# The last norm's reciprocal root: from GpSimd's power to a ScalarE root and a Newton step, with the last token tile multiplied in two column halves

## The chip, the cores and the metric

The kernel runs on one core of a Trainium2 chip. The metric is device microseconds (us) of one execution of the whole program; before the change the median of three runs is 1013.2 us. The engines are PE (TensorE: matmuls, with PEld for its weight loads), DVE (VectorE), ACT (ScalarE), POOL (GpSimd) and SP (SyncE, which here only issues transfers). Each works through its own queue in order, and waits in that queue on semaphores that other engines or transfers raise.

## The reference

One layer of a latent backbone: a short gated convolution, then a SwiGLU feed-forward, each behind an RMS norm that is modulated by a conditioning vector, each added to the residual, and a last RMS norm. 1024 tokens, model dimension 1024, hidden dimension 2816, all float32.

```python
def rmsnorm(x, g):
    return x * lax.rsqrt(jnp.mean(x * x, axis=-1, keepdims=True) + EPS) * g

sh1, sc1, g1, sh2, sc2, g2 = jnp.split(silu(c) @ ada_w + ada_b, 6, axis=-1)
x = x + g1 * short_conv_mixer(modulate(rmsnorm(x, norm1_g), sh1, sc1), ...)
gate, up = jnp.split(modulate(rmsnorm(x, norm2_g), sh2, sc2) @ ffn_w_in, 2, axis=-1)
x = x + g2 * ((silu(gate) * up) @ ffn_w_out)
return rmsnorm(x, final_g)
```

The change touches only the last two lines: the end of the feed-forward's output product, the residual and the last norm.

## The kernel before

**Products.** Each float32 operand is split in a high and a low half (`hi` by a cast on ACT, `lo` by a subtraction on DVE, L74), and a product takes three matmuls (`TERMS`: high by high, high by low, low by high). The large products are made in Winograd's form of Strassen's scheme: seven products of quarter matrices in place of eight.

**The output product** (matmuls on L999, sums `zP`) is the last 209 us of the program. Its seven products run in the order P1, P5, P6, P2, P7, P3, P4 (the table `PRODUCTS`). Each goes over 11 tiles `k` of half the hidden dimension, for four tiles of 128 tokens; each token tile has one PSUM bank of 128x512. The operands `a3h`, `a3l` (tokens) and `w3h`, `w3l` (weights) of two `k` at a time are loaded by SP, cast on ACT and completed on DVE, some steps ahead of PE. A product's `epilogue` for a token tile is issued while the next product's matmuls run: it works the sums into `top[t]` (tokens of the upper half) and `bot[t]` (lower half). P3's epilogue finishes the four `top` tiles during P4, P4's finishes the four `bot` tiles.

**The end.** P4 (`final`) takes the token tiles 0 to 2 as a group over all `k`, then the last tile (`t == TH - 1`) alone: 33 matmuls of 128x512 into the fourth bank, so that the epilogues of the first three tiles run beside it. Then that tile's own epilogue runs with nothing beside it: DVE multiplies by `g2` and adds the residual (`residual_part`: `mul`, `add`), ACT squares and sums (`AF.Square` with `accum_out`, L920), DVE multiplies the tile by the norm's gain `fg` into `zf` meanwhile, `rstd_sum` adds the sums of the left and the right half (`z_ss`), and `rstd_of` takes the mean and its power -0.5 in two instructions on GpSimd (`z_ms` L193, `z_r` L195). With `z_r`, DVE scales the left half (L974), ACT the right half (L977), and SP (L978) and ACT (L979) issue the two transfers to `out_dram`. The other seven tiles use `rstd_of` too. The `top` tiles' transfers are issued by GpSimd (L965).

**What sets the order.** A scheduler orders each engine's queue from the order of the program text and its own costs; `tc.issue_after(mm)` pins a piece of work behind a matmul. Waits between engines are set for a whole tile: a writer of a bank waits for the readers of that bank. At the end of the program (L1060) each engine has a DRAIN, and then all meet at a barrier, which GpSimd's queue gathers.

Of the kernel before, what the change touches and what calls it, by code (L numbers as in the profile page):

```python
# [16 lines left out]
H = 512          # tokens of a half, and the most columns of one product  # L17
GRID_W = 64
EPS = 1e-6
# (stationary, moving) halves of a float32 product: all but low * low  # L20
# [4 lines left out]
def trunk_kernel(ctx: ExitStack, tc: tile.TileContext, x, c, ada_w, ada_b, norm1_g, norm2_g,  # L25
# [4 lines left out]
    KD = D // P              # tiles of the model dimension  # L30
    KH = KD // 2
    NT = T // P              # tiles of tokens
    TH = H // P              # of them in a half
# [61 lines left out]
    def rows_of(name, vectors):  # L95
        """Vectors of 128, a row each; of each (first row, queue, source) a run of them."""
        rows = t2(name)[:, :P]
        nc.vector.memset(rows, 0.0)
        for r, queue, v in vectors:
            v = v.rearrange("o (k p) -> (o k) p", p=P)  # L100
            queue.dma_start(rows[r:r + v.shape[0], :], v)
        return rows
# [22 lines left out]
    aw = ada_w.rearrange("(k p) (j d) -> p k j d", p=P, j=6)  # L125

    class Ada:
        """Columns d0..d0+w of nj of the six vectors from j0: first each partition's own rows of
        ada_w, then their sum over the partitions."""
# [35 lines left out]
        def columns(self, i, g, scale, shift):  # L165
            """g * (1 + scale) and shift of its i-th tile of the model dimension, as columns."""
            ps, k, j0 = self.ps[i], self.d0 // P + i, self.j0
            nc.vector.tensor_scalar(scale[:, k:k + 1], ps[:, 1:2], ab1[:, (j0 + 1) * KD + k:(j0 + 1) * KD + k + 1],
                                    g[:, k:k + 1], op0=ALU.add, op1=ALU.mult)
            nc.vector.tensor_scalar(shift[:, k:k + 1], ps[:, 0:1], ab[:, j0 * KD + k:j0 * KD + k + 1], None, op0=ALU.add)  # L170

        def row(self, to, bias=False):
            """The sums, to their rows in DRAM; of one vector with its bias."""
# [36 lines left out]
    xT = [[t_s(f"xT{h}_{kp}", [P, 2, H]) for kp in range(KH)] for h in range(2)]  # L210

    class Tokens:
# [5 lines left out]
        def squares(self):  # L218
            # the squares themselves go where the other half's tokens come later
            self.ss = tiny(f"x{self.t}_ss")  # L220
            nc.scalar.activation(xT[1][self.i].rearrange("p k t -> p (k t)"), self.x, AF.Square, accum_out=self.ss)
# [38 lines left out]
    # ---- the convolution's input product, channels in partitions; its first channel tiles take the  # L260
    # first half of the tokens as the columns of scale and shift arrive ----
    C0 = 2
    JS = (2, 1, 0)          # hv, gate_c, gate_b
# [27 lines left out]
    def convolve(ct, u, cv):  # L291
        """Rows of the grid in u; taps of channel tile ct."""
# [9 lines left out]
    def gated0(ct, h):  # L302
        """gate_c * hv of a first channel tile and a half of the tokens."""
        u = first[ct, h] = t2(f"u{ct}_{h}")
        nc.scalar.copy(u, ps0[ct, 2, h])
        mul(u, ps0[ct, 1, h], u)
# [8 lines left out]
    # A: tokens by dimension, B: its dimension by two tiles of columns; 1 and 2 are halves.  # L315
    class Pair:
        """The products of two tiles of columns."""
# [16 lines left out]
        def weights(self, tile=t_wop):  # L334
            (b11, b21), (b12, b22) = [(raw[:, :KH, :], raw[:, KH:, :]) for raw in self.raw]
            sub(b11, b12, b11)                      # T1
            self.weight("P5", b11, tile)
            self.weight("P3", b22)
            sub(b12, b22, b12)                      # T3
            sub(b22, b22, b11)                      # T2  # L340
            self.weight("P6", b22, tile)
            self.weight("P7", b12, tile)
            sub(b21, b21, b22)                      # -T4
# [20 lines left out]
        def after(self, name, ps):  # L364
# [4 lines left out]
            elif name == "P6":  # L369
                nc.scalar.copy(self.u2, ps)                     # P1 + P6  # L370
            elif name == "P7":
                self.u3 = t2(f"u3_{self.name}")
                nc.scalar.copy(self.u3, ps)                     # P1 + P6 + P7
# [15 lines left out]
    def in_turn(pairs, count, between=None):  # L389
        """Pairs one after the other, but a product of the next one in between where one of a pair  # L390
        waits for its bank's sum to be read; the last one has its own products there."""
# [20 lines left out]
    class Mix(Pair):  # L412
        """Channel tiles ct and ct + 1 of hv (2), gate_c (1) or gate_b (0)."""
# [49 lines left out]
    def operands(raw):  # L463
        """The sums of quarters, from raw tiles by half of the tokens; what they are needed in order."""
# [5 lines left out]
        for kp in range(2):  # L470
            sub(s1[kp], s1[kp], raw[0][kp])                             # S2
            operand("S2", kp, s1[kp])
        yield
        for kp in range(2):
            sub(raw[1][kp], raw[0][kp], raw[1][kp])                     # S3
            operand("S3", kp, raw[1][kp])
        yield
        for kp in range(2):
            sub(raw[0][kp + 2], raw[0][kp + 2], s1[kp])                 # S4
# [10 lines left out]
    with in_order(ENG.SP, ENG.DVE, ENG.Activation, ENG.PE):  # L490
# [41 lines left out]
        while r:  # L532
            then = piece() if spans else None
            n = KD // len(p.ks)         # rows of the next piece to each of these
# [67 lines left out]
    def finish_piece(p=None):  # L602
        """After a product of p."""
# [50 lines left out]
    def v_tile(t, parts):  # L654
        """All channels of a tile of tokens, loaded where its low half comes."""
# [111 lines left out]
    # The output product's operands: a half of the tokens by tiles of the hidden dimension.  # L767
# [17 lines left out]
    def spill_sums(i):  # L785
        a, at = acts.pop(i), acts.pop(i + FH)
        sx, sy = t_s(f"asx_{i}", [P, 2, H]), t_s(f"asy_{i}", [P, 2, H])
        add(sx[:, 0, :], a[:, 1, :], at[:, 1, :])               # S1
        sub(sx[:, 1, :], sx[:, 0, :], a[:, 0, :])               # S2
        sub(sy[:, 0, :], a[:, 0, :], a[:, 1, :])                # S3  # L790
        sub(sy[:, 1, :], at[:, 0, :], sx[:, 1, :])              # S4
# [46 lines left out]
    queued = []  # L838

    def load(o, src):  # L840
        """In this order on their queue."""
# [7 lines left out]
    def wsource(pname, k, n):  # L849
        """The raw weight quarter of a product, for tiles k..k+n of the hidden dimension; T1 is there ahead of P5."""  # L850
# [9 lines left out]
        if pname == "P2":  # L860
            o = part("21")
            sub(tchain[k], o, tchain[k])                     # -T4
# [3 lines left out]
        if pname == "P7":  # L866
            o = part("22")
            sub(o, o, part("12"))                            # T3
            return o
        if pname == "T1":  # L870
            tchain[k] = part("12", t_s)
            sub(tchain[k], tchain[k], raw11.pop(k))          # T1, for P5
        elif pname == "P6":
            sub(tchain[k], part("22"), tchain[k])            # T2
# [31 lines left out]
    # The rows of C of a tile of tokens in each half: (C11, C12) and (C21, C22), from their parts.  # L906
# [8 lines left out]
    def residual_part(t, z, to, x1, cols):  # L915
        """x1 + g2 * z and its sum of squares."""
# [5 lines left out]
    parts = cst.tile([P, 2 * NT], F32, name="parts")          # sums of squares: left, then right halves  # L922
# [6 lines left out]

    def rstd_sum(t):  # L930
        s = tiny(f"z{t}_ss")
        add(s, parts[:, 2 * t:2 * t + 1], parts[:, 2 * t + 1:2 * t + 2])
        return rstd_of(s, f"z{t}")

    def epilogue(pname, t, z):
# [6 lines left out]
        elif pname == "P6":  # L942
            nc.scalar.copy(top[t][:, R], z)                               # P1 + P6
        elif pname == "P2":
            add(top[t][:, L], z, top[t][:, L])                            # C11
            add(top[t][:, R], top[t][:, R], bot[t][:, R])                 # P1 + P6 + P5
            if t < 2:
                top_left(t)
        elif pname == "P7":
            nc.scalar.copy(bot[t][:, L], z)                               # P1 + P6 + P7  # L950
            x1 = x1b[t] = x1_part(t + TH, "x1", slice(0, D), t_s)
            zr = bot[t][:, R]
            add(zr, bot[t][:, L], zr)                                     # C22
# [4 lines left out]
        elif pname == "P3":  # L958
            zr = top[t][:, R]
            add(zr, z, zr)                                                # C12  # L960
# [4 lines left out]
            nc.gpsimd.dma_start(out[t * P:(t + 1) * P, :], top[t])  # L965
        else:                                                             # P4: z is C21
            zl, rows = bot[t][:, L], out[(t + TH) * P:(t + TH + 1) * P]
            residual_part(t + TH, z, zl, x1b[t][:, L], L)
            if t == TH - 1:
                zf = t2("zf")  # L970
                mul(zf, zl, fg[:, L])
            r = rstd_sum(t + TH)
            if t == TH - 1:
                nc.vector.tensor_scalar(zl, zf, r, None, op0=ALU.mult)  # L974
            else:
                nc.vector.scalar_tensor_tensor(zl, zl, r, fg[:, L], op0=ALU.mult, op1=ALU.mult)
            nc.scalar.mul(bot[t][:, R], bot[t][:, R], r)  # L977
            nc.sync.dma_start(rows[:, L], zl)  # L978
            nc.scalar.dma_start(rows[:, R], bot[t][:, R])  # L979
# [3 lines left out]
    for pname in PRODUCTS:  # L983
# [12 lines left out]
        def steps(t, k):  # L996
            a, w = ops[k // 2]
            for i, (ai, wi) in enumerate(TERMS):
                mm = nc.tensor.matmul(zs[t], lhsT=a[ai][:, k % 2, t * P:(t + 1) * P], rhs=w[wi][:, k % 2, :],  # L999
# [5 lines left out]
        for k, n in ksteps:  # L1005
# [13 lines left out]
            if pname == "P6" and k == 4:  # L1019
                g2, fg = t_s("g2", [P, D]), t_s("fg", [P, D])  # L1020
                load(g2, g_rows[1][0].broadcast_to([P, D]))
                load(fg, final_g.rearrange("(o d) -> o d", o=1).broadcast_to([P, D]))
        low(FH - 1)
# [4 lines left out]
        if final:  # L1028
            for t in range(group):
                epilogue(pname, t, zs[t])  # L1030
            with tc.issue_after(mm):
                for k in range(FH):
                    steps(TH - 1, k)
            epilogue(pname, TH - 1, zs[TH - 1])
# [30 lines left out]
```

## Time and profile before

| | us |
|---|---|
| runs (three) | 1011.79, 1013.2, 1013.22; median 1013.2 |
| span of the profiled execution | 1010.4 |
| PE busy in the span | 983.7 (97%) |
| DVE / ACT / POOL busy | 724.5 / 443.6 / 90.4 |
| PE on L999, share of the chain that ended last | 21% |

The profiled execution has no time of its own beside its span; the span is 2.8 us below the median of the runs. PE works nearly throughout, so most of the program's length is PE's; the last matmul begins at 996.36 us. An engine's rows give a start, a duration, the line, the operation, and the output and inputs by the program's names; "idle before <-releaser" is what its engine waited for.

### The profile page before, as it was taken

Reading aid. Unit: us, or ns where it says so; the run is one execution under the profiler, and the core shown is the slowest. Engines: PE = TensorE matmul, PEld = TensorE weight load, DVE = VectorE, ACT = ScalarE, POOL = GpSimd, SP = SyncE. Lnnn points to the kernel's source line nnn. Section 1 sums busy time; section 2 is a strip of 40 time slices with the busy share of each in tenths; the row PEclk is TensorE's granted clock in tenths of the full one; section 3 lists DMA queues with packets and bytes.
Section 4 is the critical chain, followed back from the end, with each engine's and each line's share of the span. In section 5 each row is a group of like instructions: output and inputs, shape, how many; then the busy total and the mean of one; then the engine's idle time right before and its main releaser. Section 6 shows DMA issues by size and latency. Waiting matters only on the chain.

```text
span 1010.4 us, 12038 instructions
## 1 busy us (share of the span) xinstructions
PE 983.7 (97%) x4395; PEld 812.8 (80%) x4395; DVE 724.5 (72%) x1051; ACT 443.6 (44%) x711; POOL 90.4 (9%) x172
## 2 busy tenths in 40 slices
PE   5999999999999999999999999999999999999994
PEld 5788888887888878888888888888888888888883
DVE  6879798887945799677665665665665765777973
ACT  7684333333535575243333333333333353634642
POOL 2010000000011110110110110110110100000021
PEclk8999999999999999999999999999999999999997
DMA  9921456443875232454431431431326954578432
GB/s 308 354 68 57 128 149 208 123 149 121 250 219 182 84 105 84 137 176 135 146 115 53 146 115 53 146 115 53 126 74 218 378 183 147 187 260 294 145 134 104
DMA packets 137386, 157.36 MB, mean 156 GB/s; under 512 B 6724, under 2 KB 100016, under 8 KB 137328
## 3 DMA queue, kind: packets, MB, share of 16 engines
q1 hardware_dynamic: 126944, 124.27, 39.2%
q0 software_dynamic: 9728, 31.26, 8.4%
q10 hardware_dynamic: 656, 1.08, 0.3%
q8 instruction: 34, 0.56, 0.2%
q14 instruction: 24, 0.20, 0.1%
HBM read 123.80 MB, written 32.78 MB: 155 GB/s over the span
## 4 chain that ended last, share of the span: by engine, by line
PE 90%; DVE 4%; DMA 2%; SPq 1%; issue 1%; ACT 1%; POOL 0%; POOLq 0%; ACTq 0%; DVEq 0%
PE X_f L356 23%; PE zP L999 21%; PE Z_f L356 12%; PE X_m L356 8%; PE y L670 7%; PE Y_f L356 6%; PE u L286 6%; PE Z_m L356 4%; PE Y_m L356 2%; DMA ada_w<-in_ada_w_dram 1%; DVE ada_acc L152 1%; PE x1T L643 1%; DVE BP_f L74 1%; SPq L140 1%; DMA wr_m<-in_conv_w_in_dram 1%
## 5 line engine op out<-in xcount | busy, mean ns | idle before, releaser
L74 DVE TENSOR_TENSOR BP_f<-wr_f,BP_f 128x512 fp32r<-128x512 f32 x154 | 104.8, 688 | 60.7 <-ACT BP_f L83 58.9
L83 ACT CAST BP_f<-wr_f 128x512 fp32r<-128x512 f32 x154 | 93.9, 621 | 85.2 <-PE Z_f L356 51.6
L999 PE MATMUL zP<-w3l_P,a3h_P 128*128 128x512 f32 x308 | 119.8, 389 | 0.0
L999 PE MATMUL zP<-w3h_P,a3l_P 128*128 128x512 f32 x308 | 119.8, 389 | 0.0
L999 PE MATMUL zP<-w3h_P,a3h_P 128*128 128x512 f32 x308 | 118.4, 389 | 0.0
L999 PEld LDWEIGHTS zP<-w3l_P,a3h_P 128*128 128x128 f32 x308 | 57.8, 188 | 12.1
L999 PEld LDWEIGHTS zP<-w3h_P,a3l_P 128*128 128x128 f32 x308 | 57.8, 188 | 12.0
L999 PEld LDWEIGHTS zP<-w3h_P,a3h_P 128*128 128x128 f32 x308 | 57.8, 188 | 11.9
L74 DVE TENSOR_TENSOR a3l_P<-a3l_P,a3h_P 128x1024 fp32r<-128x1024 f32 (+1 forms) x42 | 47.3, 1133 | 27.8 <-ACT a3h_P L889 27.8
L83 ACT CAST BP_m<-wr_m 128x512 fp32r<-128x512 f32 x63 | 37.7, 620 | 59.0 <-DVE wr_m L74 32.2
L152 DVE SCALAR_TENSOR_TENSOR ada_acc<-ada_w,cols,ada_acc 128x512 f32<-128x512 f32 (+1 forms) x88 | 61.7, 711 | 2.4 <-ACT ada_acc L148 0.8
L356 PE MATMUL X_f<-A11h,BP_f 128*128 128x512 f32 x176 | 57.7, 390 | 0.0
L356 PE MATMUL X_f<-AS3h,BP_f 128*128 128x512 f32 x176 | 57.7, 389 | 0.0
L356 PE MATMUL X_f<-AS2h,BP_f 128*128 128x512 f32 x176 | 57.6, 389 | 0.0
L356 PE MATMUL X_f<-A22h,BP_f 128*128 128x512 f32 x176 | 57.6, 389 | 0.0
L356 PE MATMUL Z_f<-AS4h,BP_f 128*128 128x512 f32 x176 | 57.6, 389 | 0.0
L356 PE MATMUL Y_f<-A12h,BP_f 128*128 128x512 f32 x176 | 57.5, 389 | 0.0
L356 PE MATMUL Z_f<-AS1h,BP_f 128*128 128x512 f32 x176 | 57.4, 389 | 0.0
L74 DVE TENSOR_TENSOR BP_m<-wr_m,BP_m 128x512 fp32r<-128x512 f32 x63 | 42.4, 688 | 14.5 <-ACT BP_m L83 14.1
L670 PE MATMUL y<-woh,vh_t 128*128 128x512 f32 x128 | 50.4, 394 | 0.0
L670 PE MATMUL y<-woh,vl_t 128*128 128x512 f32 x128 | 49.9, 390 | 0.0
L670 PE MATMUL y<-wol,vh_t 128*128 128x512 f32 x128 | 49.9, 390 | 0.0
(273 smaller groups left out, 2239.1 us busy)
## 6 DMA issues: line engine op xcount, KB each, us to landing
wr_f<-in_ffn_w_in_dram SPq DMA_DIRECT2D x44, 512.0 KB, 4.1
ada_w<-in_ada_w_dram SPq DMA_DIRECT2D x64, 256.0 KB, 5.9
w_P<-in_ffn_w_out_dram SPq DMA_DIRECT2D x30, 512.0 KB, 5.7
a3l_P<-ad_S SPq DMA_DIRECT2D x20, 512.0 KB, 6.5
wr_m<-in_conv_w_in_dram SPq DMA_DIRECT2D x18, 512.0 KB, 5.3
ad<-a POOLq DMA_DIRECT2D x33, 256.0 KB, 2.6
ada_w<-in_ada_w_dram SPq DMA_DIRECT2D x16, 512.0 KB, 3.9
a3l_P<-ad SPq DMA_DIRECT2D x15, 512.0 KB, 3.8
```

Source lines behind the costliest of these rows:

```text
L74: return nc.vector.tensor_tensor(o, a, b, op=ALU.subtract)
L83: nc.scalar.copy(hi, raw)
L140: self.last_load = nc.sync.dma_start(raw[:, :, j, :], aw[:, k0:k0 + kk, j0 + j, d0:d0 + w]).ins
L152: nc.vector.scalar_tensor_tensor(acc, self.rows[k], by, acc, op0=ALU.mult, op1=ALU.add)
L286: nc.tensor.matmul(ps0[ct, j, h], lhsT=w0[k][wi][:, j, ct * P:(ct + 1) * P], rhs=h_of(k, h)[hi], start=(k == 0 and i == 0), stop=(k == KD ...
L356: mm = nc.tensor.matmul(ps, lhsT=w[:, wi, 2 * kp + kk, :], rhs=A[aname, kp][hi][:, kk, :], start=(first and kp == 0 and kk == 0 and i == 0 ...
L643: nc.tensor.transpose(ps2[:, i * P:(i + 1) * P], xn[:, k * P:(k + 1) * P], ident)
L670: mm = nc.tensor.matmul(ys[t][n], lhsT=vt[t][vi][:, k, :], rhs=wo[k][wi][:, n * H:(n + 1) * H], start=(k == 0 and i == 0), stop=(k == KD - ...
L999: mm = nc.tensor.matmul(zs[t], lhsT=a[ai][:, k % 2, t * P:(t + 1) * P], rhs=w[wi][:, k % 2, :], start=(fresh and k == 0 and i == 0), stop= ...
```

## The change

- `rstd_sum` adds the two sums and `D * EPS` in one DVE instruction, and `rsqrt` makes the reciprocal root: ACT's `Sqrt` (L940), then on DVE a reciprocal, `r * r * s`, `1.5 - 0.5 *` that, and a product (one Newton step). For eight tiles that is 8 instructions of 128x1 on ACT, 40 on DVE in place of 8, and none on GpSimd in place of 16. The mean's 1/D goes into `fg`, which GpSimd multiplies once by the root of D when it is loaded.
- The `top` tiles' transfers move from GpSimd's queue to ACT's.
- The last token tile's 33 matmuls of 512 columns become 66 of 256 columns: first all `k` for the left 256 columns, then all `k` for the right, in the same bank. `LastTile.half` does the residual part of each half; `rest` does the norm.

```diff
     def rstd_sum(t):
         s = tiny(f"z{t}_ss")
-        add(s, parts[:, 2 * t:2 * t + 1], parts[:, 2 * t + 1:2 * t + 2])
-        return rstd_of(s, f"z{t}")
+        nc.vector.tensor_scalar(s, parts[:, 2 * t:2 * t + 1], parts[:, 2 * t + 1:2 * t + 2], D * EPS,
+                                op0=ALU.add, op1=ALU.add)
+        return rsqrt(s, f"z{t}")
+
+    def rsqrt(s, name):
+
+        r, e = tiny(f"{name}_r"), tiny(f"{name}_e")
+        nc.scalar.activation(r, s, AF.Sqrt)
+        nc.vector.reciprocal(r, r)
+        nc.vector.scalar_tensor_tensor(e, r, r, s, op0=ALU.mult, op1=ALU.mult)
+        nc.vector.tensor_scalar(e, e, -0.5, 1.5, op0=ALU.mult, op1=ALU.add)
+        mul(r, r, e)
+        return r
...
-            nc.gpsimd.dma_start(out[t * P:(t + 1) * P, :], top[t])
+            nc.scalar.dma_start(out[t * P:(t + 1) * P, :], top[t])
...
+    class LastTile:
+
+
+        def __init__(self, t, zs):
+            self.t, self.zs, self.zf = t, zs, t2("zf")
+            self.ss, self.sums = [tiny(f"zl_ss{i}") for i in range(2)], tiny("zl_sums")
+
+        def half(self, i):
+            c = slice(i * H // 2, (i + 1) * H // 2)
+            t, z, x1 = self.t, bot[self.t][:, c], x1b[self.t][:, c]
+            mul(z, self.zs[i][:, c], g2[:, c])
+            add(z, z, x1)
+            nc.scalar.activation(x1, z, AF.Square, accum_out=self.ss[i])
+            mul(self.zf[:, c], z, fg[:, c])
+            if i == 0:
+                right = 2 * (t + TH) + 1
+                nc.vector.tensor_scalar(self.sums, self.ss[0], parts[:, right:right + 1], D * EPS,
+                                        op0=ALU.add, op1=ALU.add)
+
+        def rest(self):
+            t, s = self.t, tiny("zl_s")
+            rows = out[(t + TH) * P:(t + TH + 1) * P]
+            add(s, self.ss[1], self.sums)
+            r = rsqrt(s, "zl")
+            nc.vector.tensor_scalar(self.zf, self.zf, r, None, op0=ALU.mult)
+            nc.scalar.mul(bot[t][:, R], bot[t][:, R], r)
+            nc.sync.dma_start(rows[:, L], self.zf)
...
+                nc.gpsimd.tensor_scalar(fg, fg, D ** 0.5, None, op0=ALU.mult)
...
         if final:
             for t in range(group):
                 epilogue(pname, t, zs[t])
-            with tc.issue_after(mm):
-                for k in range(FH):
-                    steps(TH - 1, k)
-            epilogue(pname, TH - 1, zs[TH - 1])
+            last = LastTile(TH - 1, [zs[TH - 1]] * 2)
+            for i in range(2):
+                with tc.issue_after(mm):
+                    for k in range(FH):
+                        mm = steps(TH - 1, k, cols=slice(i * H // 2, (i + 1) * H // 2))
+                last.half(i)
+            last.rest()
```

Where the instructions stand now, at three places. The first is GpSimd's queue from the last spill of the feed-forward's activations (L795) to the end of the program, as a piece of the difference (the part for the tiles z2 to z7 repeats what is shown).

```order
 L778 DMA ad_3072<-a_6234 128x512
 L795 DMA ad_S_3077<-asy_6245 128x512
-L193 TENSOR_SCALAR z_ms<-z_ss 128x1
-L195 TENSOR_TENSOR z_r<-z_ms,mhalf 128x1
-L965 DMA out_dram<-top_6492 128x1024
...
-L1060 UNCONDITIONAL_BRANCH
-L1060 ISA
+L1059 TENSOR_SCALAR fg<-fg 128x1024
+L1100 UNCONDITIONAL_BRANCH
+L1100 ISA
```

GpSimd's last work of its own is now the scaling of `fg`, which stands in the middle of the output product; the norms and the four transfers are gone from its queue. The second place is the seam between the two column halves, first on PE (`zP_3` is the last tile's bank, `_10` the last `k`, `_0` the first).

```order
L1034 MATMUL zP_3_6243<-w3h_P_10_7748,a3h_P_10_7744 128x256
L1034 MATMUL zP_3_6243<-w3l_P_10_7749,a3h_P_10_7744 128x256
L1034 MATMUL zP_3_6243<-w3h_P_10_7748,a3l_P_10_7745 128x256
L1034 MATMUL zP_3_6243<-w3h_P_0_7561,a3h_P_0_7557 128x256 [waits DVE_49]
L1034 MATMUL zP_3_6243<-w3l_P_0_7562,a3h_P_0_7557 128x256
```

PE's first matmul of the right columns now waits for DVE, for the instruction that reads the left columns out of the shared bank; before, no matmul of the last tile had such a wait. That instruction stands in DVE's queue here (fifth row below; `bot_6692` and `bot_6730` are the tiles 0 and 1, `bot_6811` the last; the `z` names are the norms' 128x1 columns).

```order
L943 TENSOR_SCALAR z_e<-z_e 128x1 [waits DVE_49]
L80 TENSOR_TENSOR z_r<-z_r,z_e 128x1 [waits DVE_49]
L982 SCALAR_TENSOR_TENSOR bot_6692<-bot_6692,z_r,fg 128x512 [waits DVE_49]
L941 RECIPROCAL z_r<-z_r 128x1 [waits Activation_49]
L80 TENSOR_TENSOR bot_6811<-zP_3_6243,g_6732 128x256 [waits PE_49]
L942 SCALAR_TENSOR_TENSOR z_e<-z_r,z_ss 128x1 [waits DVE_49]
```

It comes behind the first tile's norm and the second one's reciprocal, and ahead of the rest of the second one's. The third place is ACT's queue in the middle of P4 (`w3h_P_10` is the last weight cast that PE needs; `top_6492` is tile 0, `top_6562` tile 2).

```order
L889 CAST a3h_P_10_7744<-a3l_P_10_7745 128x512 [waits DMAHW3_49,PE_49,Activation_49]
L883 CAST w3h_P_10_7748<-w_T_12_10_6433 128x512 [waits PE_49]
L940 ACT_TABLE_LOAD
L940 ACTIVATE z_r<-z_ss 128x1 [waits DVE_49] x2
L920 ACTIVATE x1r_7682,parts<-top_6562 128x512 [waits DMAHW0_49,DVE_49]
L976 ACTIVATE top_6492<-top_6492,z_r 128x512 [waits DVE_49]
L977 DMA out_dram<-top_6492 128x1024 [waits DVE_49,Activation_49]
```

Before, the first `top` tile's scaling followed the last weight cast directly; now a load of ACT's function table and two roots stand between, and a transfer's issue behind it.

## Rows read from the trace of the kernel before

**Rows 1.** The page: the length of the profiled execution.
```profile
span 1010.4 us, 12038 instructions
```

**Rows 2.** Busy time in three stretches of the end; idle engines show 0.00.
```profile
core 0: us, PE busy (x) PEld busy (x) DVE busy (x) ACT busy (x) POOL busy (x), PEclk, DMA share, GB/s
...
1001.00:1004.00 3.00, 0.00 (x0) 0.00 (x0) 0.00 (x0) 0.00 (x0) 0.00 (x0) 0.50 0.47 175
1004.00:1008.00 4.00, 0.00 (x0) 0.00 (x0) 0.00 (x0) 0.00 (x0) 0.00 (x0) 0.50 0.00 0
1008.00:1010.40 2.40, 0.00 (x0) 0.00 (x0) 0.00 (x0) 0.00 (x0) 0.00 (x0) 0.50 0.00 0
```

**Rows 3.** The program's last line, L1060: ns min/median/max, first and last start in us.
```profile
L1060 POOLq DRAIN  x3: 46/112/10152, 999.5 to 1010.2; - x3
L1060 SPq DRAIN  x3: 7/7/7, 1003.7 to 1009.9; - x3
L1060 PEldq DRAIN  x2: 13/2140/4267, 992.5 to 1010.0; - x2
L1060 DVEq DRAIN  x2: 19/272/526, 1000.1 to 1009.9; - x2
```

**Rows 4.** SP's waits from 985 us on: us in total, times, longest.
```profile
SPq L1060 <- PEq L1060: 6.6, 2, 6.1
```

**Rows 5.** Timeline of the last token tile: start, duration, engine, line, operation.
```profile
989.11 0.39 PE L999 MATMUL zP<-w3h_P,a3h_P 128*128 128x512 f32 x1
...
992.57 0.75 DVE L976 SCALAR_TENSOR_TENSOR bot<-bot,z_r,fg 128x512 f32<-128x512 f32 x1 [0.73 <-POOL z_r L195]
...
996.36 0.39 PE L999 MATMUL zP<-w3h_P,a3l_P 128*128 128x512 f32 x1
...
996.79 0.69 DVE L80 TENSOR_TENSOR bot<-zP,g 128x512 f32<-128x512 f32 x1 [0.22 <-PE zP L999]
997.51 0.69 DVE L77 TENSOR_TENSOR bot<-bot,x 128x512 f32<-128x512 f32 x1
998.24 0.63 ACT L920 ACTIVATE x<-bot 128x512 f32<-128x512 f32 x1 [1.70 <-DVE bot L77]
...
998.77 0.19 ACT L920 ACTIVATION_READ_ACCUMULATOR x<-bot 128x1 f32 x1
998.99 0.16 DVE L77 TENSOR_TENSOR z_ss<-parts 128x1 f32<-128x1 f32 x1
...
999.52 0.55 POOL L195 TENSOR_TENSOR z_r<-z_ms,mhalf 128x1 f32<-128x1 f32 x1
1000.10 0.72 ACT L977 ACTIVATE bot<-bot,z_r 128x512 f32<-128x512 f32 x1 [1.14 <-POOL z_r L195]
...
1000.85 0.34 ACTq L979 DMA_DIRECT2D out_dram<-bot  x1
```

**Rows 6.** Timeline of PE at two earlier places with short matmuls.
```profile
26.25 1.84 PE L161 MATMUL ada_ps<-ones,ada_acc 128*128 128x1 f32 x16
...
371.66 1.09 PE L643 MATMUL x1T<-ident,xr 128*128 128x128 f32 x8 [1.01 <-DVE xr L695]
```

**Rows 7.** Timeline of ACT at the program's start: a table load and a small cast.
```profile
0.72 1.28 ACT L115 ACT_TABLE_LOAD   x1 [0.72 <-PEq L1051]
...
2.02 0.19 ACT L115 CAST ones_r<-ones 128x1 fp32r<-128x1 f32 x1
```

**Rows 8.** Line L168 on DVE, 128x1 with PSUM and pointer operands: ns min/median/max.
```profile
L168 DVE TENSOR_SCALAR scale<-ada_ps,ab,cols x8: 272/278/279, 15.9 to 47.6; 128x1 f32<-128x1 f32 x8
```

**Rows 9.** Tile fg: its load by SP and its first use by DVE.
```profile
L80 DVE TENSOR_TENSOR top<-top,fg x4: 684/692/693, 910.3 to 947.7; 128x512 f32<-128x512 f32 x4
...
L843 SPq DMA_DIRECT2D fg<-in_final_g_dram x1: 384/384/384, 817.5 to 817.5; - x1
```

**Rows 10.** Timeline of P4: ACT's last weight cast.
```profile
970.50 0.62 ACT L883 CAST w3h_P<-w_T 128x512 fp32r<-128x512 f32 x1
```

**Rows 11.** Timeline of P4: DVE's low half of the weights for k = 8.
```profile
980.09 1.22 DVE L74 TENSOR_TENSOR w3l_P<-w_T,w3h_P 128x1024 fp32r<-128x1024 f32 x1
```

More of the change, by code (lines that the diff above doesn't have):

```diff
@@ L968, in epilogue @@
             residual_part(t + TH, z, zl, x1b[t][:, L], L)
-            if t == TH - 1:
-                zf = t2("zf")
-                mul(zf, zl, fg[:, L])
             r = rstd_sum(t + TH)
[L973 to L976, printed above, removed]
+            nc.vector.scalar_tensor_tensor(zl, zl, r, fg[:, L], op0=ALU.mult, op1=ALU.mult)
             nc.scalar.mul(bot[t][:, R], bot[t][:, R], r)
             nc.sync.dma_start(rows[:, L], zl)
+            nc.scalar.dma_start(rows[:, R], bot[t][:, R])
+    class LastTile:
[21 more added lines that the diff above has]
+            nc.sync.dma_start(rows[:, L], self.zf)
             nc.scalar.dma_start(rows[:, R], bot[t][:, R])
@@ L994, in low, with steps @@
                 low3(*operand3)
-        def steps(t, k):
+        def steps(t, k, to=None, cols=slice(None)):
             a, w = ops[k // 2]
             for i, (ai, wi) in enumerate(TERMS):
-                mm = nc.tensor.matmul(zs[t], lhsT=a[ai][:, k % 2, t * P:(t + 1) * P], rhs=w[wi][:, k % 2, :],
+                mm = nc.tensor.matmul((zs[t] if to is None else to)[:, cols],
+                                      lhsT=a[ai][:, k % 2, t * P:(t + 1) * P], rhs=w[wi][:, k % 2, cols],
                                       start=(fresh and k == 0 and i == 0), stop=(k == FH - 1 and i == 2),
```

## The prediction

> **What bounds the kernel now.** PE works through nearly the whole program, so I read the end first, where PE has stopped. The timeline of the last token tile [rows 5] shows one chain with nothing beside it: PE's last matmul begins at 996.36; DVE, ACT, DVE, GpSimd, then DVE and ACT take turns until ACT issues the last transfer at 1000.85. The busy times by stretch [rows 2] say when this is over: no engine works after 1001, and after 1004 no DMA either; both stretches up to the end show zeros. Yet the span goes to 1010.4 [rows 1]. So about 6.7 us at the end hold no work at all.
>
> The program's last line says what fills them [rows 3]. SP's DRAIN, behind SP's waits for the last landing, is at 1003.7: the outputs are in DRAM. GpSimd's DRAIN starts at 999.5, while its last power runs, and takes 10.152 us: it ends at 999.5 + 10.15 = 1009.65. From there to the end of the span are 1010.4 - 1009.65 = 0.8 us of barrier. SP waits 6.1 us on that line [rows 4]; the name given there is PE's queue, but PE's DRAIN is long over (992.5 + 4.27 = 996.8, the end of its last matmul), and DVE's too (1000.1 + 0.53 = 1000.6, the end of its last scaling). These two also tell what a DRAIN follows: its own engine's last work, not the end of the program. Only GpSimd's ends late: 9.6 us after its power (999.52 + 0.55 = 1000.07). GpSimd is thus what ends the program, by a tail that no busy time shows.
>
> **Part 1: GpSimd's late work goes.** Its last work becomes the scaling of `fg`, loaded from 817.5 and first used at 910.3 [rows 9]. No row shows a 128x1024 scaling on GpSimd; between nothing and the 87 us that remain if the load takes as long as 5 us, it costs nothing, since only DVE at 910.3 waits for it. The DRAIN then stands behind work of about 825 us, and even 10 us of it are over 160 us before the end. The end is then SP's DRAIN plus the barrier: 1003.7 + 0.8 = 1004.5 if all else stayed, a gain of 5.9 us. Below follows what the rest takes back of it.
>
> **Part 2: the last tile on PE.** Before, 33 matmuls from 989.11 to 996.36: (996.36 - 989.11) / 32 = 0.227 us each; DVE begins 0.43 us after the last start, 0.20 beyond its slot [rows 5]. What one of 256 columns takes is not shown. Half of 0.227 is 0.113, if only columns count. The short ones with a weight load each give a floor for the load: 16 of one column in 1.84 us, 8 of 128 in 1.09, so 0.115 to 0.136, the long tail of the last one counted in [rows 6]. From above it is bounded by the 0.227 of 512 columns. I take 0.120, nearest to both floors. That is 66 x 0.120 = 7.92 in place of 33 x 0.227 = 7.48: +0.44 us (at 0.113: 0; at 0.136: +1.5).
>
> The seam adds a wait. The last matmul of the left columns begins at 989.11 + 32 x 0.120 = 992.95, so DVE could read at 993.27. DVE is then in tile 0's scaling, until 992.57 + 0.75 = 993.32 before [rows 5]; its reciprocal root comes at about the same time as GpSimd's did (Part 3), and one more reciprocal is ahead, so I let it read at 993.4. A multiplication of 256 columns is 0.42 (0.69 for 512 columns, 0.16 for one: halfway [rows 5]). PE begins the right columns at 993.4 + 0.42 + 0.03 = 993.85 in place of 993.07: 0.8 us lost. Behind that wait PE has only the 33 matmuls; the bound below is 0.55, if DVE were free at once. The last one begins at 993.85 + 3.84 = 997.69, and DVE at 997.69 + 0.32 = 998.01, in place of 996.79: **+1.2 us**. DVE is free by then: from 993.85 on it has about 4.0 us of rows of 0.16 to 0.75, which overlap by some 0.07 each (two tiles' scalings and root steps, the left half's add and gain), and ends near 997.5, half a microsecond ahead; this margin is thin.
>
> **Part 3: the chain behind it.** Before, from DVE's 996.79 to the end of ACT's issue (1000.85 + 0.34) are 4.40 us. After it is, in order: multiplication 0.42; add 0.42; square 0.41 and its sum 0.09 beyond it (0.63 for 512 columns and 0.19 for one; the sum's row ends 0.72 behind the square's start) = 0.50; sum 0.16; root on ACT 0.22 (a 128x1 cast is 0.19 [rows 7]); reciprocal 0.17; the three-operand product 0.22 (L168, with two pointers and PSUM, is 0.28 [rows 8]); two small ones of 0.16; ACT's scaling 0.72; issue 0.34. Together 3.49, with ten handovers of 0.03 (997.51 is 0.03 behind 996.79 + 0.69) 3.79: **-0.6 us**. The two small halves save 0.27 each, the square 0.2; the Newton step loses to GpSimd: 0.93 + 0.15 against 0.95 between the sum's end (999.15) and 1000.10. For the five operations no row is exact: at 0.15 to 0.31 each the chain is 0.2 shorter to 0.5 longer. So the last issue ends at about 1001.19 + 1.2 - 0.6 = 1001.8. The transfer's bytes and queue are the same, landing and SP's DRAIN at +2.5 us, as before (1003.7 - 1001.19): 1004.3; and 0.8 of barrier: **1005.1**.
>
> **Part 4: the middle of P4.** The table load comes once, behind the last weight cast at 970.50 + 0.62 = 971.12 [rows 10]; at 1.28 us [rows 7] the first root is ready at 971.12 + 1.28 + 0.22 = 972.62. DVE's reciprocal waits for it, and behind that in its queue is `w3l` for k = 8. The 19 rows from that reciprocal to that one add up, at the durations above (0.69 for 512 columns, 1.22 for 1024, 0.75 for a scaling), to 8.6 us without overlap: 981.3, the very end of before (980.09 + 1.22 [rows 11]). PE wants it at its second matmul of k = 8, 26 slots ahead of the last tile: 989.11 - 26 x 0.227 = 983.2. That leaves 1.9 us, so it costs nothing; without that cover each us beyond would be one. The four `top` transfers on ACT's queue cost some 0.35 us of ACT each; each also waits for DVE's scaling of the same tile, and behind it stand the next tile's square and scaling, which PE does not wait for. On SP nothing moves but the last tile's.
>
> **The sum.** 1005.1 + 2.8 (the median of the runs stands at 1013.2, the span at 1010.4) = 1007.9 us, a gain of 5.3.
>
> **The rivals.** *The end is not tied to GpSimd's last work (the change does not do what it says; this ends above before).* The DRAIN would be there at each program's end and close some 6 us behind the last landing, whatever GpSimd did: it ends 1009.65 - 1003.7 = 5.95 behind SP's. It decides as soon as GpSimd's DRAIN, though early, ends late or its part of the barrier does. Then only Parts 2 and 3 count: +0.6, 1013.8 us, slower by less than can be told. For it: nothing explains why a DRAIN behind 0.55 us of work takes 10 us. Against it: it begins at 999.5 without a wait, and PE's and DVE's follow their own work. The Trainium skill has a rule on this side: its page "Runtime: NRT & Kernel Launch", section "The ~15µs preamble/postamble breakdown", tells of about 6.2 us in a profile's total that no kernel changes. By that rule the time would be the 1013.8 of this rival; SP's 6.1 us are near it in size, but the 10.15 us stand on one engine's row, with a start of its own. I give it 0.12.
>
> *Matmuls of 256 columns cost as much as 512.* If the weight load and its switch, not the columns, set the slot, it goes up to 0.227: the left half ends at 996.36, DVE reads 996.8 to 997.2, the right half ends at 997.25 + 7.25 + 0.43 = 1004.9, 6.9 us behind 998.0: 1014.8, slower by 1.6. Halfway (0.17) it is 1011.2, still faster. Against it: 128 columns with a load in 0.136 or less. 0.06.
>
> *The middle stalls.* If the table switch or the waits between ACT and DVE (five for each tile) hold `w3l` beyond 983.2, PE waits, and each us comes on top: at 3 us 1010.9. The Trainium skill, "ScalarE: Activation LUTs", section "What ACT_TABLE_LOAD costs", sets a switch at 2.66 us, a drain of 1.38 included, and would speak against a root here. The trace has the 1.28, and ACT's next work 0.02 us behind it (0.72 + 1.28 to 2.02 [rows 7]); by the page's figure the margin shrinks from 1.9 to 0.5, an estimate, and the sum stays. 0.05.
>
> **How the numbers follow.** The forecast has 0.77. Its own range: slots of 0.113 to 0.15 on PE (-0.5 to +2.0), the root -0.2 to +0.5, and the offset of the fastest run of before (1011.79, 1.4 below the median): about 1005.7 to 1010.4. To leave out no more than 2 in 10 it has to reach into the stalls and the dearer matmuls: 1005.4 to 1011.3. A difference of 0.2%, 2.0 us, is about what a measurement of this kernel can tell from none. Faster by more: the forecast, most of the stalls, a part of the dear matmuls, 0.82. Within: the end that does not move, and matmuls near 0.2, 0.13. Slower by more takes dear matmuls and a stall, or the unmoved end with either: 0.05.
>
> **What would show it.** GpSimd's DRAIN starts near 825 and no stretch of several us without work is left before the end of the span; SP's first DRAIN is near 1004.3 and the span ends 0.8 behind it. On PE the right columns begin 0.8 us late with DVE's read of the left columns named, and slots are near 0.12. The forecast is wrong if SP again waits some 6 us on the last line with all engines idle, if the last tile's slots are over 0.15, or if PE stands still for `w3l` near 983.

## The result and the profile after

The changed kernel takes 1007.22 us (median of 1006.5, 1007.39, 1007.46 and 1007.05), the kernel before 1013.0 in the runs beside it: a ratio of 0.9942, 95% interval 0.9928 to 0.9956, 5.8 us faster. The forecast was 1007.9.

The page of the profiled execution, its span and its busy times. The span fell by 5.7 us ([rows 1] had 1010.4), while PE is as busy as before (983.9 for 983.7): PE, which works through 98% of the span, was saved nothing.

```profile
span 1004.7 us, 12134 instructions
...
PE 983.9 (98%) x4428; PEld 814.1 (81%) x4428; DVE 728.0 (72%) x1087; ACT 446.8 (44%) x722; POOL 83.5 (8%) x153
```

The DRAINs of the program's last line, now L1100 (duration min/median/max in ns, first and last start in us), the answer to [rows 3]:

```profile
L1100 POOLq DRAIN  x3: 46/106/13097, 822.3 to 1004.5; - x3
L1100 SPq DRAIN  x3: 7/7/7, 1003.9 to 1004.2; - x3
```

GpSimd's long DRAIN is still there, and even longer (13.1 us), but it begins at 822.3 and is over at 835.4, 169 us before the end of the span. SP's DRAIN is at 1003.9, where it was at 1003.7, and the span ends 0.8 us behind it. SP's waits on the last line (engine, line waited for; total us, times, longest) went from 6.6 us to this:

```profile
SPq L1100 <- PEq L1100: 0.7, 2, 0.5
```

The busy times of the last stretches, columns as in [rows 2]: of the two stretches of 4.0 and 2.4 us without work, 0.7 us are left.

```profile
1001.00:1004.00 3.00, 0.00 (x0) 0.00 (x0) 0.08 (x1) 0.32 (x1) 0.00 (x0) 0.61 0.47 175
1004.00:1004.70 0.70, 0.00 (x0) 0.00 (x0) 0.00 (x0) 0.00 (x0) 0.00 (x0) 0.50 0.00 0
```

The timeline of the last tile, the answer to [rows 5] (start, duration, engine, line, operation, what ended the idle time before it). First PE, at the tile's first matmul, at the seam and at the last one, with DVE's reads of the bank:

```profile
988.94 0.28 PE L1034 MATMUL zP<-w3h_P,a3h_P 128*128 128x256 f32 x1
...
992.43 0.75 DVE L982 SCALAR_TENSOR_TENSOR bot<-bot,z_r,fg 128x512 f32<-128x512 f32 x1
992.77 0.28 PE L1034 MATMUL zP<-w3h_P,a3l_P 128*128 128x256 f32 x1
993.17 0.41 DVE L80 TENSOR_TENSOR bot<-zP,g 128x256 f32<-128x256 f32 x1
993.63 0.38 PE L1034 MATMUL zP<-w3h_P,a3h_P 128*128 128x256 f32 x1 [0.57 <-DVE bot L80]
...
997.55 0.28 PE L1034 MATMUL zP<-w3h_P,a3l_P 128*128 128x256 f32 x1
997.87 0.42 DVE L80 TENSOR_TENSOR bot<-zP,g 128x256 f32<-128x256 f32 x1 [0.60 <-PE zP L1034]
```

A matmul of 256 columns has a slot (from its start to the next one's) of (992.77 - 988.94) / 32 = 0.120 us. At the seam PE begins at 993.63 where its next slot was at 992.89: 0.74 us lost, until DVE has read the left half. Then, of the chain behind the last matmul:

```profile
998.79 0.42 ACT L999 ACTIVATE x<-bot 128x256 f32<-128x256 f32 x1 [1.77 <-DVE bot L77]
...
999.33 0.16 DVE L77 TENSOR_TENSOR zl_s<-zl_ss,zl_sums 128x1 f32<-128x1 f32 x1
999.52 0.20 ACT L940 ACTIVATE zl_r<-zl_s 128x1 f32<-128x1 f32 x1 [0.22 <-DVE zl_s L77]
999.76 0.16 DVE L941 RECIPROCAL zl_r<-zl_r 128x1 f32<-128x1 f32 x1 [0.27 <-ACT zl_r L940]
999.96 0.22 DVE L942 SCALAR_TENSOR_TENSOR zl_e<-zl_r,zl_s 128x1 f32<-128x1 f32 x1
...
1000.59 0.72 ACT L1012 ACTIVATE bot<-bot,zl_r 128x512 f32<-128x512 f32 x1 [0.87 <-DVE zl_r L80]
...
1001.35 0.34 ACTq L1014 DMA_DIRECT2D out_dram<-bot  x1
```

From DVE's read at 997.87 to the end of the issue at 1001.69 are 3.82 us, where there were 4.40.

### The profile page after: what moved, and what is told of

It is laid out like the page before. It is cut to its first block, busy times and chain, and to the rows that moved or that the text cites. A ratio compares the mean times of both kernels' runs of the same rounds, so it can differ in the third digit from the quotient of the medians.

```text
span 1004.7 us, 12134 instructions
## 1 busy us (share of the span) xinstructions
PE 983.9 (98%) x4428; PEld 814.1 (81%) x4428; DVE 728.0 (72%) x1087; ACT 446.8 (44%) x722; POOL 83.5 (8%) x153
## 4 chain that ended last, share of the span: by engine, by line
PE 90%; DVE 4%; DMA 3%; issue 1%; SPq 1%; ACT 0%; POOL 0%; ACTq 0%; DVEq 0%; POOLq 0%
PE X_f L356 23%; PE zP L1034 20%; PE Z_f L356 12%; PE X_m L356 8%; PE y L670 8%; PE Y_f L356 6%; PE u L286 6%; PE Z_m L356 4%; PE Y_m L356 2%; DMA ada_w<-in_ada_w_dram 1%; DMA w0r<-in_conv_w_in_dram 1%; PE x1T L643 1%; DVE BP_f L74 1%; DMA wr_m<-in_conv_w_in_dram 1%; DVE ada_acc L152 1%
## 5 line engine op out<-in xcount | busy, mean ns | idle before, releaser
L1034 PE MATMUL zP<-w3l_P,a3h_P 128*128 128x512 f32 (+1 forms) x319 | 121.8, 382 | 0.0
L1034 PE MATMUL zP<-w3h_P,a3l_P 128*128 128x512 f32 (+1 forms) x319 | 121.7, 382 | 0.0
L1034 PE MATMUL zP<-w3h_P,a3h_P 128*128 128x512 f32 (+1 forms) x319 | 120.4, 382 | 0.6 <-DVE bot L80 0.6
L1034 PEld LDWEIGHTS zP<-w3h_P,a3h_P 128*128 128x128 f32 x319 | 59.9, 188 | 12.3 <-DVE bot L80 0.8
L1034 PEld LDWEIGHTS zP<-w3l_P,a3h_P 128*128 128x128 f32 x319 | 60.0, 188 | 11.7
L1034 PEld LDWEIGHTS zP<-w3h_P,a3l_P 128*128 128x128 f32 x319 | 60.0, 188 | 11.6
```

The lines of the kernel that those rows point to most:

```text
L1034: mm = nc.tensor.matmul((zs[t] if to is None else to)[:, cols], lhsT=a[ai][:, k % 2, t * P:(t + 1) * P], rhs=w[wi][:, k % 2, cols], start= ...
```

## The experiments

The theory: GpSimd's DRAIN closes some 9 to 10 us behind GpSimd's last work, whatever that is; the change gains because this end is now early, and the halves of the last tile and the new root together cost a little time. The rivals: the DRAIN belongs to the power, or to the program's end; the halves are what pays. One execution can run some 2.5 us earlier or later than another long before its end (GpSimd's scaling of `fg` began between 822.1 and 824.6 us), so ends are compared within each trace, from the last tile or from SP's DRAIN. The four experiments with late work on GpSimd have one execution each, all on one chip, so their times alone could not settle differences of that size; their traces have to.

### One small late instruction on GpSimd

To the changed kernel, one GpSimd instruction of 128x1 that nobody waits for, behind the last tile's sum:

```diff
             add(s, self.ss[1], self.sums)
+            nc.gpsimd.tensor_scalar(tiny("extra"), s, 1.0 / D, EPS, op0=ALU.mult, op1=ALU.add)
             r = rsqrt(s, "zl")
```

> The changed kernel with one extra GpSimd instruction of 128x1 that nobody waits for, on the last tile's sum (there at 999.5). My theory: GpSimd's DRAIN starts behind its last work and takes about 10.15 us, as in the kernel before and in the halves alone: from 999.6 to 1009.7, the span ends 0.8 behind it at 1010.5, 5.7 us above the changed kernel's 1004.8, so 1012.3; this one small instruction gives back the whole gain. Rival 1: the long DRAIN belongs to the power, or to the eight pairs of instructions, not to any late work: then the span stays at 1004.8. Rival 2: the DRAIN closes 6 us behind the last landing whatever GpSimd does: excluded by the changed kernel's trace already, and would give 1004.8 here too.

Measured: 1013.21 us in one execution, the kernel before beside it 1012.63. GpSimd's timeline and the DRAINs on the last line:

```profile
1001.21 0.19 POOL L1010 TENSOR_SCALAR extra<-zl_s 128x1 f32<-128x1 f32 x1 [173.47 <-DVE zl_s L77]
```
```profile
L1101 POOLq DRAIN  x3: 46/106/9457, 1001.2 to 1011.2; - x3
L1101 SPq DRAIN  x3: 7/7/7, 1005.5 to 1010.9; - x3
```

This execution runs 1.7 us later than the changed kernel's from early on, which is why its time lies above that of the kernel before. Its DRAIN ends at 1001.2 + 9.46 = 1010.7, its span at 1011.4: 5.9 us behind SP's DRAIN, where it was 0.8 in the changed kernel. One instruction of 0.19 us costs 5.1 us, nearly the whole gain of the change. The power is not needed for it: rival 1 falls. It is 0.6 less than expected, since the DRAIN takes 9.46 and not 10.15 here.

The same instruction 2.2 us earlier, on the left half's sum:

```diff
+                nc.gpsimd.tensor_scalar(tiny("extra"), self.sums, 1.0 / D, EPS, op0=ALU.mult, op1=ALU.add)
```

> The same extra instruction on the left half's sum, which is there at 997.3, 2.2 us earlier. My theory: DRAIN from 997.4 to 1007.5, span 1008.3, 2.2 us less than with the instruction at 999.5 and 3.5 above the changed kernel's; time near 1010.1. Rival: if the length of the DRAIN depends on what comes after, not on its start, the span is the same as with the later one, or 1004.8.

Measured: 1011.58 us in one execution.

```profile
999.58 0.19 POOL L1005 TENSOR_SCALAR extra<-zl_sums 128x1 f32<-128x1 f32 x1 [171.18 <-DVE zl_sums L1003]
```
```profile
L1101 POOLq DRAIN  x3: 46/106/9467, 999.5 to 1009.5; - x3
L1101 SPq DRAIN  x3: 7/7/7, 1006.1 to 1009.3; - x3
```

The span (1009.8) ends 3.7 us behind SP's DRAIN, 2.9 more than the 0.8 of the changed kernel: 2.2 us less than with the instruction 2.2 us later. Counted from SP's DRAIN, the end moves with the instruction, one to one. The last landing does not close the DRAIN: that is over at 1006.1, and the DRAIN still runs to 1009.0.

And once more at 992, on the first bottom tile's root:

```diff
             r = rstd_sum(t + TH)
+            if t == 0:
+                nc.gpsimd.tensor_scalar(tiny("extra"), r, 1.0 / D, EPS, op0=ALU.mult, op1=ALU.add)
```

> The same extra instruction on the first bottom tile's reciprocal root, there at 992.4. My theory: DRAIN from 992.5 to 1002.7, which is over before SP's DRAIN at 1003.9, so nothing is lost: span within 0.5 us of 1004.8. Rival: any GpSimd work in the last stretch costs several us, however early: above 1008.

Measured: 1006.29 us in one execution, span 1004.5.

```profile
992.26 0.68 POOL L983 TENSOR_SCALAR extra<-z_r 128x1 f32<-128x1 f32 x1 [166.37 <-ACT x L920]
```
```profile
L1102 POOLq DRAIN  x3: 46/106/9942, 992.2 to 1004.2; - x3
L1102 SPq DRAIN  x3: 7/7/7, 1003.7 to 1004.0; - x3
```

The DRAIN ends at 1002.1, ahead of SP's at 1003.7, and the span 0.8 behind SP's: late work that is early enough costs nothing. Against this run the one with the instruction behind the last tile's sum takes 6.9 us longer: SP's DRAIN comes 1.8 us later there (1005.5), and the end behind it accounts for the other 5.1.

### A transfer in place of computing

The changed kernel with one of the last transfers issued by GpSimd:

```diff
-            nc.scalar.dma_start(rows[:, R], bot[t][:, R])
+            (nc.gpsimd if t == 2 else nc.scalar).dma_start(rows[:, R], bot[t][:, R])
```

> The changed kernel with one transfer (right half of the third bottom tile) issued by GpSimd in place of ScalarE, near 996.7 to 997.3; GpSimd computes nothing late. If a transfer's issue counts as work for the DRAIN: from 997.3 to 1007.5, span 1008.3. If only computing counts, the DRAIN starts and ends with the issue and the span stays near 1004.8. I lean to the first, since the change took the top transfers from GpSimd too; no trace so far tells them apart.

Measured: 1010.44 us in one execution.

```profile
997.97 0.60 POOL L985 DMA_DIRECT2D out_dram<-bot  x1 [170.74 <-ACT bot L983]
```
```profile
L1100 POOLq DRAIN  x3: 46/112/9934, 997.9 to 1008.4; - x3
L1100 SPq DRAIN  x3: 7/7/7, 1005.0 to 1008.1; - x3
```

A transfer's issue counts as work: the span (1008.7) ends 3.7 us behind SP's DRAIN, again 2.9 too many. The `top` tiles' transfers, which the change takes from GpSimd too, are early enough, however. The last of them in the kernel before:

```profile
984.01 0.61 POOL L965 DMA_DIRECT2D out_dram<-top  x1 [1.33 <-ACT top L964]
```

With 9.3 us behind its end at 984.6, the DRAIN would close near 994, ahead of SP's. By this estimate that part of the change was not needed for the gain; no run leaves these transfers on GpSimd and takes only the powers away.

All ten traces together, in us; the DRAIN's end is its start and duration added:

| kernel | GpSimd's last work ends | its DRAIN ends | between |
|---|---|---|---|
| before | 1000.07 (power) | 1009.65 | 9.6 |
| halves alone (below) | 1007.30 (power) | 1016.85 | 9.6 |
| changed | 826.19 (128x1024 scaling, 3.82 us) | 835.4 | 9.2 |
| changed, again | 825.18 (the same, 2.79 us) | 834.4 | 9.2 |
| in one piece (below) | 826.89 (the same, 3.71 us) | 836.1 | 9.2 |
| two banks (below) | 825.25 (the same, 2.79 us) | 834.5 | 9.2 |
| small, at 1001.2 | 1001.40 | 1010.66 | 9.3 |
| small, at 999.6 | 999.77 | 1008.97 | 9.2 |
| small, at 992.3 | 992.94 | 1002.14 | 9.2 |
| transfer | 998.57 | 1007.83 | 9.3 |

It is the time behind the last work's end that stays nearly the same, not the DRAIN's own length: where the scaling took 1.0 us less, the DRAIN was 1.0 us shorter. The scaling in the changed kernel, then the scaling and the DRAIN in its second trace (to be held against the 13097 ns above):

```profile
822.37 3.82 POOL L1059 TENSOR_SCALAR fg<-fg 128x1024 f32<-128x1024 f32 x1 [31.76 <-PE zP L1034]
```
```profile
822.39 2.79 POOL L1059 TENSOR_SCALAR fg<-fg 128x1024 f32<-128x1024 f32 x1 [31.71 <-PE zP L1034]
...
L1100 POOLq DRAIN  x3: 46/102/12074, 822.3 to 1004.5; - x3
```

### The last tile in one piece

The changed kernel without the halves; the root and GpSimd's early end stay. The edit of the loop (a second piece, not shown, lets `epilogue` multiply this tile by `fg` into a tile of its own beside the square, as in the kernel before):

```diff
-            last = LastTile(TH - 1, [zs[TH - 1]] * 2)
-            for i in range(2):
-                with tc.issue_after(mm):
-                    for k in range(FH):
-                        mm = steps(TH - 1, k, cols=slice(i * H // 2, (i + 1) * H // 2))
-                last.half(i)
-            last.rest()
+            with tc.issue_after(mm):
+                for k in range(FH):
+                    steps(TH - 1, k)
+            epilogue(pname, TH - 1, zs[TH - 1])
```

> The changed kernel with its last token tile multiplied in one piece again (33 matmuls of 512 columns, one epilogue); the root on ScalarE, the Newton step and GpSimd's early end stay. My theory: the halves cost more on PE (66 slots of 0.12 and 0.74 us at the seam, together 1.2 us) than they save behind it (two DVE steps of 0.27 and 0.21 of the square, 0.75 us), so without them the kernel is 0.5 us faster than the changed one: 1006.7 us if that is at 1007.2, DVE reading the last tile near 996.6, SP's first DRAIN near 1003.4. Rival: the halves pay, because the chain is what ends the program and PE's extra is hidden: then it is 0.7 us slower than the changed kernel, 1007.9.

Beside it on the same chip, the changed kernel again:

> The changed kernel itself, beside the others on the same chip: 1007.2 us, GpSimd's DRAIN from 822.3, SP's first DRAIN near 1003.9, the span ending 0.8 us behind it.

Measured: 1006.65 us (1006.5 to 1006.74) without the halves, 1006.58 (1006.3 to 1007.18) with them, 1012.51 before; ratios to before 0.9941 (0.9928 to 0.9953) and 0.9942 (0.993 to 0.9954). The runs don't tell the two apart. The trace without halves:

```profile
989.65 0.39 PE L1040 MATMUL zP<-w3h_P,a3h_P 128*128 128x512 f32 x1
...
997.33 0.69 DVE L80 TENSOR_TENSOR bot<-zP,g 128x512 f32<-128x512 f32 x1 [0.27 <-PE zP L1040]
...
1001.60 0.34 ACTq L991 DMA_DIRECT2D out_dram<-bot  x1
```

This execution reached the last tile 0.7 us later than the changed kernel's. From the tile's first matmul to the end of the last issue it takes 1001.94 - 989.65 = 12.3 us, with halves 1001.69 - 988.94 = 12.75. So the halves cost 0.45 us in the trace, near the 0.5 expected, which five runs cannot show. The kernel before took 1001.19 - 989.11 = 12.08 for the same stretch, so the new root costs the other 0.2 us. What the runs settle is that the whole gain is there without the halves. The rival, that they pay 0.7 us, has the trace against it and two medians that are 0.07 us apart.

### The right half in a bank of its own

```diff
+        def ahead(self):
+            c = slice(H // 2, H)
+            z, x1 = bot[self.t][:, c], x1b[self.t][:, c]
+            mul(z, z, g2[:, c])
+            add(x1, z, x1)
...
-            last = LastTile(TH - 1, [zs[TH - 1]] * 2)
+            right = bank("zR")
+            last = LastTile(TH - 1, [zs[TH - 1], right])
+            last.ahead()
...
```

The pieces that are not shown send the right half's matmuls to the second bank and start that bank from zero.

> The changed kernel with the right half of the last tile in a bank of its own: the bank starts from zero, and the sum that the first bank held (P1 + P6 + P7, already copied to bot) is multiplied and added to the residual ahead of time. PE then has no wait at the seam. My theory: the 0.74 us at the seam are on the path; 0.13 us of them come back because DVE's sum of the left half, which waits for ScalarE, stands in front of its read of the right half: 0.6 us faster than the changed kernel, 1006.6 if that is at 1007.2, no idle time of PE at the first matmul of the right half. Rival: DVE and ScalarE are the bound there (two tiles' norms are queued ahead), and the time stays within 0.2 us of the changed kernel's.

Measured: 1006.06 us (1005.82 to 1007.84), ratio to before 0.994 (0.9926 to 0.9953). PE at the seam, and DVE ahead of the right half's read:

```profile
993.05 0.28 PE L1040 MATMUL zP<-w3h_P,a3l_P 128*128 128x256 f32 x1
993.17 0.28 PE L1040 MATMUL zR<-w3h_P,a3h_P 128*128 128x256 f32 x1
...
997.01 0.28 PE L1040 MATMUL zR<-w3h_P,a3l_P 128*128 128x256 f32 x1
...
997.33 0.21 DVE L1009 TENSOR_SCALAR zl_sums<-zl_ss,parts 128x1 f32<-128x1 f32 x1 [0.40 <-ACT x L1005]
997.46 0.41 DVE L80 TENSOR_TENSOR bot<-zR,g 128x256 f32<-128x256 f32 x1
```

PE goes from one bank to the other in its ordinary 0.12 us. DVE's read then comes right behind its sum of the left half, which waited 0.40 us for ScalarE. PE's last matmul begins at 997.01, and 0.32 us behind that, as in the changed kernel (997.55 to 997.87), DVE could have read at 997.33: the next limit takes back 0.13 us, as expected. With the tile's first matmul 33 slots of 0.12 ahead of 993.17, at 989.2, the span (1004.3) ends 15.1 us behind it; in the changed kernel 1004.7 - 988.94 = 15.8. The 0.7 us are what the seam cost, less those 0.13. It is the fastest kernel by its median, 0.5 us below the changed one, but one of its five runs lies above all of that one's: the runs don't tell these two apart either.

### The halves alone

The kernel before, with the last tile in halves and the norms and transfers left on GpSimd (the edit of the loop and `LastTile` as in the change, with `rstd_of` for the root):

> The kernel before with only the last tile's two column halves; the norms' power and the four top transfers stay on GpSimd. My theory: DVE's read of the left half stands behind the scaling of the third tile, which waits for GpSimd's power until 995.8, so it comes at 996.6 instead of 993.2, PE stands 3.3 us at the seam, and GpSimd's last power and the 10 us behind it move with it: about 3.4 us slower than before, 1016.4. Rival: the halves are worth what their shorter chain saves, and the time is within 0.5 us of before's 1013.0.

Measured: 1018.16 us (1017.83 to 1019.63), ratio to before 1.0058 (1.0044 to 1.0071). The tile's first matmul, PE's wait at the seam, what DVE did ahead of its read, and GpSimd's DRAIN:

```profile
991.19 0.28 PE L1032 MATMUL zP<-w3h_P,a3h_P 128*128 128x256 f32 x1
...
995.02 0.28 PE L1032 MATMUL zP<-w3h_P,a3l_P 128*128 128x256 f32 x1
...
997.89 0.75 DVE L981 SCALAR_TENSOR_TENSOR bot<-bot,z_r,fg 128x512 f32<-128x512 f32 x1 [0.71 <-POOL z_r L195]
...
998.55 0.42 DVE L80 TENSOR_TENSOR bot<-zP,g 128x256 f32<-128x256 f32 x1
...
999.03 0.39 PE L1032 MATMUL zP<-w3h_P,a3h_P 128*128 128x256 f32 x1 [3.73 <-DVE bot L80]
```
```profile
L1097 POOLq DRAIN  x3: 46/107/10152, 1006.7 to 1017.4; - x3
```

The mechanism is the expected one: DVE's queue has the read behind the third tile's scaling, that waits for GpSimd's power, and PE stands for 3.73 us. The amount is not: 5.65 us in place of 3.4. This trace is of the slowest of the four runs (1019.63 us) and reaches the last tile 2.1 us later than the kernel before did; from the tile's first matmul to the end of the span (1017.7) it takes 26.5 us, in the kernel before 21.3, so 5.2 us are lost there. The seam costs 3.9 us (999.03 for a slot at 995.14), 0.6 more than expected, where DVE's read itself, 0.45 us, had been left out. Most of the rest is PE's clock. Windows of 1 us (PE, PEld, DVE, ACT and POOL busy, then the granted clock, DMA share and GB/s):

```profile
999.00:1000.00 1.00, 0.97 (x7) 0.97 (x8) 0.85 (x2) 0.51 (x2) 0.00 (x0) 0.93 1.00 365
1000.00:1001.00 1.00, 1.00 (x7) 1.00 (x6) 0.16 (x1) 0.00 (x0) 0.00 (x0) 0.50 0.93 344
...
1002.00:1003.00 1.00, 1.00 (x6) 1.00 (x6) 0.00 (x0) 0.00 (x0) 0.00 (x0) 0.50 0.00 0
1003.00:1004.00 1.00, 1.00 (x10) 1.00 (x9) 0.00 (x0) 0.00 (x0) 0.00 (x0) 0.87 0.00 0
```

After the wait PE ran at full clock at first, and then at half of it (1.2 in place of 2.4 GHz): its slots went from 0.12 to 0.21 us between 999.85 and 1003.25, 16 slots that took 3.40 us in place of 1.92, 1.5 us more. In the changed kernel the clock stayed up through the short wait at the seam:

```profile
993.00:994.00 1.00, 0.43 (x4) 0.38 (x4) 1.00 (x7) 0.29 (x2) 0.00 (x0) 1.00 0.00 0
```

That the length of the wait brought the clock down is thus argued from two traces, not shown by a run that changes nothing else.

## Why the prediction was right

- **Where the end comes from.** Right, and now shown: GpSimd's DRAIN held the program's end, and its end follows GpSimd's last work. The step "the end is SP's DRAIN plus 0.8" holds (1003.9 + 0.8 = 1004.7). The first rival, a tail that the kernel cannot move, is out: the last wait of SP shrank to 0.5 us. The rule of the Trainium skill that stood on its side, in "Runtime: NRT & Kernel Launch", section "The ~15µs preamble/postamble breakdown", may tell of another total, which no run here shows; these 6 us were the kernel's.
- **Part 1.** The scaling of `fg` took 3.82 us and 2.79 in the second trace; hidden, as said.
- **Part 2.** Slots of 0.120 as taken; the forecast had picked this between 0.113 and 0.136, so that it fits to the last digit is in part luck. The seam cost 0.74 for 0.8, and DVE read the right half 8.93 us behind the tile's first matmul where it was 7.68: +1.25, for +1.2. The second rival (dear matmuls) is out.
- **Part 3.** 3.82 us for 3.79. The operations without a row came out at 0.20 (root), 0.16 (reciprocal) and 0.22.
- **Part 4.** The table load took 1.28 us and stalled nothing: on L1034 PE waits once from 960 us on, for the 0.6 us at the seam. The load and the root in ACT's timeline, and the end of the weights' low half on DVE:

```profile
970.83 1.28 ACT L940 ACT_TABLE_LOAD   x1
972.13 0.20 ACT L940 ACTIVATE z_r<-z_ss 128x1 f32<-128x1 f32 x1
```
```profile
978.35 1.20 DVE L74 TENSOR_TENSOR w3l_P<-w_T,w3h_P 128x1024 fp32r<-128x1024 f32 x1
```

  The root comes 0.02 us behind the load; the 1.38 us of drain that the Trainium skill adds ("ScalarE: Activation LUTs", "What ACT_TABLE_LOAD costs") are not in this trace. The low half was ready at 979.6 and not at 981.3: the sum without overlap was too long by 1.7 us, on the safe side.
- **What was off.** Two terms, both too long. The landing: SP's DRAIN came 2.2 us behind the last issue's end, not 2.5. And the offset from span to time: 2.8 us were taken from the median of runs and the span of one execution that need not belong together. In the runs after, each time has its own span, and they are 1.8 us apart (1006.5 and 1004.7, 1007.46 and 1005.7; before, 1012.75 and 1010.9); the other 1.0 would be how far the profiled execution of the kernel before lay below its median, and no run shows a time for that one. The span forecast, 1005.1, lies within the four spans measured (1004.7 to 1005.7); with 1.8 it would have given 1006.9. The profiled execution, 1006.5, is the fastest of the four, 1.4 below the forecast; that the median of 1007.22 comes within 0.7 of it is in part luck, since the median lies above the profiled execution after the change too.

The forecast named GpSimd's end as the gain and the halves as a small loss, and both hold. It did not see that the halves need the rest of the change: alone they cost 5.65 us, because DVE's read of the left half then stands behind a scaling that waits for GpSimd's power, where in the changed kernel it comes at 993.2. Whether another order of DVE's queue would have spared them that was not run.

## What to carry to other kernels

Look at the end of a program for time in which no engine works, and for the engine whose DRAIN ends last: here it was GpSimd that held the end, and its busy time did not show it. In this program GpSimd's last instruction, a transfer's issue included, has to end 9 to 10 us ahead of the last landing; what counts is when it ends, not how long it works (0.19 us of work cost 5.1). And before an accumulation is cut in two in one bank, look in whose queue its reader stands: PE waits for all that is ahead of it there (3.73 us in the halves alone).

## What the runs showed of the hardware

- GpSimd's DRAIN at the program's end closes 9.2 to 9.6 us behind the end of its last work, in ten traces, for a power, a scaling of 128x1 or 128x1024, and a transfer's issue. What it does in that time no row shows; why it is 9.6 behind a power and 9.2 to 9.3 behind the others was not tried.
- PE's granted clock stayed at 1.00 through a wait of 0.57 us at the seam; behind one of 3.73 us it was at 1.00 for some 0.8 us and then at 0.50 for 3.4 us of uninterrupted matmuls: the 16 matmuls at the lower level took 1.5 us more than at the higher. This is one trace; the wait as the cause is argued.
